# Fill pieces of a token mixer, traced at a lower scheduling priority than the delta rule they are mixed with

## The chip, the cores and the metric

The kernel runs on one core of a Trainium2 chip. It computes two transformer blocks, one behind the other, for one sequence of 256 tokens and a model width of 1024, all in float32. The metric is device time in microseconds; the kernel before takes 939.88 us (median of 3 runs, 939.13 to 941.12).

## The reference, cut to what matters

The change touches only the token mixer of the first block. The projection of the normed input is split into attention's q, k, v (8 heads of 64), the delta rule's q, k, v (`gdn_qkv`), a gate z and two scalars per head. Attention and the gated delta rule are independent of each other until `w_out` reads both.

```python
h = rms_norm(x, pre_mix_norm[l])
proj = jnp.einsum('bsd,dc->bsc', h, w_in[l])
att_q, att_k, att_v, gdn_qkv, gdn_z, gdn_a, gdn_b = jnp.split(proj, split_points, axis=-1)
o_att = moba_attention(...)          # one causal softmax block, relative bias
o_gdn = gated_deltanet(gdn_qkv, gdn_z, gdn_a, gdn_b, ...)
mix = jnp.einsum('bsc,cd->bsd', jnp.concatenate([o_att, o_gdn], axis=-1), w_out[l])
...
# gated_deltanet, chunks of 64 tokens (4 of them):
qkv = causal_depthwise_conv_silu(qkv, conv_w)
q = l2_normalize(q) * dh ** -0.5;  k = l2_normalize(k)
m = jnp.where(strict, jnp.einsum('bhnid,bhnjd->bhnij', k_beta, kc) * decay, 0.0)
uw = lax.linalg.triangular_solve(m + eye, rhs, lower=True, unit_diagonal=True)
attn_intra = jnp.einsum('bhnid,bhnjd->bhnij', qc, kc) * decay
def step(state, xs):                 # sequential over the 4 chunks
    v_new = u_c - w_c @ state
    o = q_c @ state + a_c @ v_new
    state = state * gl + k_c.T @ v_new
o = o * lax.rsqrt(jnp.mean(o * o) + EPS) * norm_w * silu(z)
```

The rest of the first block (an MLP of width 4096) and the whole second block follow and are as before.

## The kernel before, in words

**Weights.** Every large product is computed in three float32r passes: a weight tile arrives by DMA (`raw`, L214, 512 KB, issued by SyncE), ScalarE writes its rounded high part (`wh`), VectorE the rest (`wl`), and TensorE multiplies `wh` with the activations' high and low parts and `wl` with the high part. The buffers rotate: 3 of `raw`, 6 each of `wh` and `wl`. So a DMA for a weight tile can be issued when the tile three places earlier has been split, and a `wh` can be written when TensorE has used the one six places earlier.

**Two streams.** The mixer is written as two streams. The main stream is the delta rule, written out in `body` from the call `go(FILL[0])` on: gates, normed k and q, the product matrix, a triangular solve (blocks of 16 by GpSimd, `tb` and `ub`, through DRAM; then two levels, 16 and 32, by TensorE), `us` and `wt` from the solved matrix, and the scan over four chunks. The other stream is the generator `fill()`: the projections for conv q, k, v (`qkv(i)`), attention's q and k (`att_in`), z, v (`v_in`), attention's logits, softmax, transposed probabilities and output, and two steps of `w_out`. The main stream calls `go(amount)` between its own steps; `go` pulls pieces out of `fill()` until their planned microseconds (the yielded numbers) reach the amount, or until a named point ("k", "q", "v", "z") is passed. The table `FILL` holds the amounts.

**What sets the order.** The instructions are traced into a framework that schedules them: it gives each traced instruction a priority number that counts up (`tc.cur_priority`), simulates the engines with its own estimates, and writes a fixed list for each engine, at each step the instruction with the lowest number among those it takes for ready. On the chip each engine runs its list in that order. `issue_after` (the helper `after`, L171) pins a few instructions behind others.

**Names.** A tile's name ends in a trace counter. `mm_`, `sd_`, `at_` are PSUM banks: `mm` (3 banks) for projections, `sd` (3) for the delta rule, `at` (2) for attention. In the order: `raw_254`, `raw_257`, `raw_260`, `raw_267` and their `wh_`, `wl_` are z's four weight tiles (outputs `mm_252`, `mm_253`); `raw_281`, `raw_284` are those of attention's second k (`mm_280`); `raw_320` and so on v's (`mm_318`, `mm_319`). `aqk` are attention's q and k, `lg` its logits and probabilities, `pt` the transposed probabilities, `mixh`, `mixl` its output split for `w_out` (`mm_350` to `mm_352` and `at_353`, which keeps one of the two `at` banks from then on). `m` is the product matrix, `md` its copy in DRAM, `mb` its blocks on GpSimd, `td`, `ud` the solved blocks in DRAM, `T`, `U` what is read back, `Q` the middle products of a solve level, `st` the state, `ro` and `og` the output's norm and the output.

**The steps that the prediction speaks of.** GpSimd's block solve is L898 to L905; its result is written at L906 and L907 and read back at L954. The two levels are the loop at `for si, s in enumerate((16, 32))`, `us` and `wt` the loop behind it, and the scan the loop `for t in range(2)` behind `late = iter(())`; `gdn_out` normalises one half of the output. Attention's `logits`, `probs_T` and `att_out` are called only from `fill()`.

Of the kernel before, what the change touches and what calls it, by code (L numbers as in the profile page):

```python
# [31 lines left out]
TAIL_R = ((0, 3), (1, 3))  # L32
TAIL_O = ((0, 5), (1, 5))
YR_OFF = 1
WBUFS = 6
RBUFS = 3
GATE_H = ("sq", "xh", "xh")
# [62 lines left out]
def body(ctx: ExitStack, tc: tile.TileContext, I: dict, cst: bass.AP, out: bass.AP, dbg=None):  # L100
# [16 lines left out]
    def nm(s):  # L117
        uid[0] += 1
        return f"{s}_{uid[0]}"
# [51 lines left out]
    @contextmanager  # L171
    def after(what):

        if what in last:
            with tc.issue_after(last[what].ins):
                yield
        else:
            yield
# [33 lines left out]
    def load_w(w, k0, nk, c0, ncol):  # L212
        raw = wpool.tile([P, nk, ncol], F32, tag="raw", name=nm("raw"), bufs=RBUFS)
        last["ld"] = nc.sync.dma_start(raw, w[k0 * P:(k0 + nk) * P, c0:c0 + ncol].rearrange("(k p) n -> p k n", p=P))  # L214
        H = wpool.tile([P, nk, ncol], F32R, tag="wh", name=nm("wh"), bufs=WBUFS)
        L = wpool.tile([P, nk, ncol], F32R, tag="wl", name=nm("wl"), bufs=WBUFS)
        n = len(started)
# [50 lines left out]
    def put_off(f, n):  # L268

        later.append([n, f])  # L270
# [418 lines left out]
    def go(what):  # L689

        while what not in passed if isinstance(what, str) else what > 0:
            c = next(side, None)
            if c is None:
                return
            if isinstance(c, str):
                passed.add(c)
            elif not isinstance(what, str):
                what -= c
# [7 lines left out]


    go(FILL[0])
    load_consts(0, NMIX)
    pc = sdps()  # L710
# [5 lines left out]
    last["ld"] = nc.sync.dma_start(raw, w_in[:, 3584:3600].rearrange("(k p) n -> p k n", p=P))  # L716
    HL = wpool.tile([P, 8, 32], F32R, tag="wh", name=nm("wh"), bufs=WBUFS)
    with after("xh"):
# [34 lines left out]
    dump("beta", beta)  # L753

    go("k")
    last["yk"] = last["y"]

# [21 lines left out]
    mm(pg[:, 16:32], C("aft"), g)  # L779
    mm(pg[:, 32:64], ones, gm)  # L780
    go(FILL[1])

    def tok_major(i0, t):
# [404 lines left out]
    def yr_T(h):  # L1188
        yr.grow(4, "yr", "tg")
        for j in range(2):  # L1190
            ps = sdps()
            for i in range(2):
                f = 2 * j + i
                for t in range(2):
                    nc.tensor.transpose(ps[:, i * S + t * P:i * S + (t + 1) * P],  # L1195
                                        RN[t][h][:, f * P:(f + 1) * P], ident)
            for i in range(2):
                f = 4 * h + 2 * j + i
                v = ps[:, i * S:(i + 1) * S]
                hv, lv = yr.at(f)  # L1200
                act(hv, v, AF.Copy, scale=gret(f))
                stt(lv, v, gret(f), hv.bitcast(F32), MUL, SUB)

    for h in range(4):
# [22 lines left out]
        if h:  # L1227
            yr_T(h - 1)
    put_off(lambda: yr_T(3), YR_OFF)

# [155 lines left out]
```

## Time and profile before

| | |
|---|---|
| time, median of 3 runs | 939.88 us |
| profiled execution: time / span | 941.93 / 940.0 us |
| mean granted clock of TensorE | 0.993 |
| TensorE busy | 913.8 us (97%) |
| VectorE / ScalarE / GpSimd busy | 559.6 (60%) / 453.2 (48%) / 94.4 us (10%) |
| TensorE on the chain that ended last | 86% |

The mixer is the first fifth of the span: the first transposes of the normed input for the MLP come at 197.8 us. A time is read against the profiled execution's span and what lies around it (1.9 us). In a timeline, "idle before <-releaser" tells how long the engine had nothing to run and what ended that.

### The profile page before, as it was taken

What the parts mean: (1) busy time and instruction counts of PE and PEld (TensorE: products, weight loads), DVE (VectorE), ACT (ScalarE), POOL (GpSimd) and SP (SyncE); (2) the same over time, 40 slices, a digit from 0 to 9 for tenths busy, and PEclk for the clock granted to TensorE, in tenths of its full rate; (3) what the DMA queues carried; (4) which work ended last, traced back from release to release, by engine and by line L of the source; (5) the groups of instructions that cost most, each with busy time, mean ns of one, the idle gap of its engine ahead of it and who ended that gap; (6) DMA issues with size and microseconds to landing.
All of it is one profiled execution on the core that took longest, in us unless ns stands there. A gap on an engine that the chain in (4) does not pass through costs nothing.

```text
span 940.0 us, 15151 instructions
## 1 busy us (share of the span) xinstructions
PE 913.8 (97%) x6096; PEld 812.4 (86%) x6096; DVE 559.6 (60%) x770; ACT 453.2 (48%) x639; POOL 94.4 (10%) x127
## 2 busy tenths in 40 slices
PE   7797999999999999999999999999999999999997
PEld 7697887778999888799988899988888789999886
DVE  3776535486766544768666675645457656555443
ACT  4744464256655443654545554345344545444432
POOL 4187001130000000203200000000000000000000
PEclk9999899999999999999999999999999999999999
DMA  8685542156765666577645466566474567665551
GB/s 216 183 198 148 146 157 90 45 162 174 215 189 190 215 192 197 155 217 210 181 115 176 133 176 184 163 209 191 157 235 142 172 194 201 186 187 185 182 177 45
DMA packets 176870, 161.98 MB, mean 172 GB/s; under 512 B 18916, under 2 KB 144152, under 8 KB 176800
## 3 DMA queue, kind: packets, MB, share of 16 engines
q1 hardware_dynamic: 174912, 155.96, 56.6%
q0 software_dynamic: 1728, 4.78, 1.6%
q8 instruction: 48, 0.79, 0.4%
q10 hardware_dynamic: 160, 0.27, 0.1%
q14 instruction: 22, 0.18, 0.0%
HBM read 158.07 MB, written 2.92 MB: 171 GB/s over the span
## 4 chain that ended last, share of the span: by engine, by line
PE 86%; DMA 4%; DVE 4%; ACT 2%; issue 2%; POOL 1%; SPq 0%; POOLq 0%; ACTq 0%; DVEq 0%
PE mm L230 71%; PE at L230 8%; PE sd L230 7%; DMA raw<-in_w_in_dram 3%; DVE wl L149 1%; DVE acc L152 1%; ACT wh L146 1%; PE sd L802 1%; DMA hs<-in_dec_b_dram 1%; DMA raw<-in_w_up_dram 1%; ACT junk L405 0%; PE sd L1195 0%; POOL r L410 0%; POOL rnk L149 0%; POOL rnq L149 0%
## 5 line engine op out<-in xcount | busy, mean ns | idle before, releaser
L149 DVE TENSOR_TENSOR wl<-raw,wh 128x1024 fp32r<-128x1024 f32 x285 | 348.4, 1227 | 263.5 <-ACT wh L146 262.2
L146 ACT ACTIVATE wh<-raw 128x1024 fp32r<-128x1024 f32 x287 | 302.2, 1056 | 352.3 <-PE mm L230 125.6
L230 PE MATMUL mm<-xTh,wh 128*128 128x256 f32 x960 | 273.1, 286 | 0.2
L230 PE MATMUL mm<-xTl,wh 128*128 128x256 f32 x960 | 272.4, 285 | 0.3 <-DVE xTl L475 0.2
L230 PE MATMUL mm<-xTh,wl 128*128 128x256 f32 x960 | 268.8, 285 | 0.0
L230 PEld LDWEIGHTS mm<-xTl,wh 128*128 128x128 f32 x960 | 185.3, 193 | 1.6 <-DVE xTl L475 0.7
L230 PEld LDWEIGHTS mm<-xTh,wh 128*128 128x128 f32 x960 | 185.2, 193 | 0.8 <-ACT xTh L474 0.6
L230 PEld LDWEIGHTS mm<-xTh,wl 128*128 128x128 f32 x960 | 183.4, 193 | 0.7 <-issue 0.5
L230 PE MATMUL mm<-wh,xTh 128*128 128x512 f32 x264 | 104.0, 394 | 1.2 <-ACT xTh L394 1.2
L230 PE MATMUL mm<-wh,xTl 128*128 128x512 f32 x264 | 103.2, 391 | 1.5 <-DVE xTl L397 1.5
L230 PE MATMUL mm<-wl,xTh 128*128 128x512 f32 x264 | 103.3, 391 | 0.0
L230 PE MATMUL mm<-wh,hidh 128*128 128x512 f32 x162 | 63.3, 391 | 0.1
L230 PE MATMUL mm<-wl,hidh 128*128 128x512 f32 x162 | 63.3, 391 | 0.0
L230 PE MATMUL mm<-wh,hidl 128*128 128x512 f32 x162 | 63.0, 389 | 0.0
L230 PEld LDWEIGHTS mm<-wh,xTl 128*128 128x128 f32 x264 | 49.6, 188 | 12.9 <-DVE xTl L397 2.8
L230 PEld LDWEIGHTS mm<-wh,xTh 128*128 128x128 f32 x264 | 49.6, 188 | 12.3 <-ACT xTh L394 1.9
L230 PEld LDWEIGHTS mm<-wl,xTh 128*128 128x128 f32 x264 | 49.6, 188 | 10.4 <-DVE wl L149 0.5
L410 POOL TENSOR_TENSOR r<-ms,neghalf 128x1 f32<-128x1 f32 x13 | 9.8, 757 | 462.0 <-DVE ms L152 462.0
L230 PEld LDWEIGHTS mm<-wh,hidl 128*128 128x128 f32 x162 | 30.4, 188 | 6.4
L230 PEld LDWEIGHTS mm<-wh,hidh 128*128 128x128 f32 x162 | 30.5, 188 | 6.3 <-issue 0.5
L230 PEld LDWEIGHTS mm<-wl,hidh 128*128 128x128 f32 x162 | 30.5, 188 | 5.6
L405 ACT ACTIVATE junk<-x 128x512 f32<-128x512 f32 x18 | 11.3, 626 | 18.7 <-DVE x L149 12.9
(374 smaller groups left out, 1149.8 us busy)
## 6 DMA issues: line engine op xcount, KB each, us to landing
raw<-in_w_in_dram SPq DMA_DIRECT2D x116, 512.0 KB, 4.5
raw<-in_w_up_dram SPq DMA_DIRECT2D x32, 512.0 KB, 4.5
raw<-in_w_down_dram SPq DMA_DIRECT2D x32, 512.0 KB, 4.3
raw<-in_w_ff_gate_dram SPq DMA_DIRECT2D x22, 512.0 KB, 4.0
raw<-in_w_ff_up_dram SPq DMA_DIRECT2D x22, 512.0 KB, 4.5
raw<-in_w_ff_down_dram SPq DMA_DIRECT2D x22, 512.0 KB, 3.6
raw<-in_w_r_out_dram SPq DMA_DIRECT2D x16, 512.0 KB, 3.8
raw<-in_w_out_dram SPq DMA_DIRECT2D x8, 512.0 KB, 3.5
```

Source lines behind the costliest of these rows:

```text
L146: nc.scalar.activation(o, i, f, **kw)
L149: (eng or nc.vector).tensor_tensor(o, a, b, op=op)
L152: nc.vector.scalar_tensor_tensor(o, a, s, b, op0=op0, op1=op1)
L230: nc.tensor.matmul(o, a, b, start=start, stop=stop)
L405: last["sq"] = nc.scalar.activation(T2("junk", tag="j"), srcs[i], AF.Square, scale=1.0 / 32, accum_out=ss[:, i:i + 1])
L410: last["pow"] = nc.gpsimd.tensor_tensor(r, ms, neghalf[:, :1], op=ALU.pow)
L802: nc.tensor.transpose(ps[:, a * P:(a + 1) * P], src[:, a * P:(a + 1) * P], ident)
```

## The change

Each time `go` asks the fill generator for its next piece, it first raises the framework's priority counter by 4000 and lowers it again afterwards. Everything that the piece traces (loads, splits, matmuls, evictions, attention's vector work) so gets a number 4000 higher, behind every instruction of the delta rule; the counter at the end of the mixer is near 2100. What is computed, the pieces, their amounts and the buffers are as before.

```diff
 YR_OFF = 1
+LOW = 4000
 WBUFS = 6
...
         while what not in passed if isinstance(what, str) else what > 0:
+            tc.cur_priority += LOW
             c = next(side, None)
+            tc.cur_priority -= LOW
             if c is None:
```

The number of matmuls is the same; ScalarE gets two more table loads (ACT_TABLE_LOAD) in the mixer. Order differs on all engines from the start of the mixer to its end, and hardly behind it. Three places show how.

SyncE's list, where the solved blocks (`td`, `ud`) are written and read back (`U`, `T`), before:

```order
L906 DMA td_451<-tb_147_751 128x16x16
L907 DMA ud_452<-ub_148_752 128x16x16
L214 DMA raw_257_1400<-in_w_in_dram 128x2x512
L214 DMA raw_260_1418<-in_w_in_dram 128x2x512
L214 DMA raw_267_1474<-in_w_in_dram 128x2x512
L954 DMA U_213_1140<-ud_452 64x8x64 x2
L954 DMA T_212_1139<-td_451 64x8x64 x2
```

and now:

```order
L909 DMA td_451<-tb_147_751 128x16x16
L910 DMA ud_452<-ub_148_752 128x16x16
L215 DMA raw_260_1418<-in_w_in_dram 128x2x512
L215 DMA raw_267_1474<-in_w_in_dram 128x2x512
L215 DMA raw_281_1547<-in_w_in_dram 128x8x128
L215 DMA raw_284_1577<-in_w_in_dram 128x8x128
L957 DMA U_213_1140<-ud_452 64x8x64 x2
L957 DMA T_212_1139<-td_451 64x8x64 x2
```

One weight load (`raw_257`) has moved ahead of the write, and two (`raw_281`, `raw_284`) have moved from behind the reads to ahead of them.

TensorE's list, from the second level of the solve (`sd_263`), before (36 matmuls of z come ahead of it, 12 stand between `sd_265` and `sd_272`, of which three are shown):

```order
L230 MATMUL sd_263_1436<-U_241_1333,b_152_792 64x64 x16
L230 MATMUL sd_265_1455<-U_243_1352,b_154_796 64x64 x16
L230 MATMUL mm_252_1380<-wh_268_1476,xTh_25_165 128x512
L230 MATMUL mm_252_1380<-wl_269_1477,xTh_25_165 128x512
L230 MATMUL mm_252_1380<-wh_268_1476,xTl_29_169 128x512
```

and now:

```order
L231 MATMUL sd_263_1436<-U_241_1333,b_152_792 64x64 x16
L231 MATMUL sd_265_1455<-U_243_1352,b_154_796 64x64 x16
L231 MATMUL sd_272_1496<-Q_264_1453,T_237_1295 64x64 x16
L231 MATMUL sd_274_1515<-Q_266_1472,T_239_1314 64x64 x16
L231 MATMUL sd_300_1647<-vb_200_1062,U_273_1513 64x64 x16
L231 MATMUL sd_303_1667<-U_273_1513,kbe_124_645 64x64 x8
L231 MATMUL sd_304_1677<-U_273_1513,kbe_124_645 64x64 x8
L231 MATMUL sd_305_1687<-vb_202_1069,U_275_1532 64x64 x16
L231 MATMUL sd_308_1707<-U_275_1532,kbe_126_649 64x64 x8
L231 MATMUL sd_309_1717<-U_275_1532,kbe_126_649 64x64 x8
L231 MATMUL sd_317_1736<-us_301_1664,kd_125_646 128x128 x4
L231 MATMUL sd_316_1735<-us_301_1664,at_180_914 64x64 x8
```

The level, `us`, `wt` and the scan's first chunk stand in one piece; before, fill matmuls stood between most of them.

TensorE's list at attention's last head pair (1, 1), from the second transposes of its probabilities (`at_365`) to its output (`at_368`), before:

```order
L632 MATMUL at_365_1955<-ident_80,lg1_339_1863 128x128 x2
L230 MATMUL sd_360_1945<-st_315_1732,qdt_174_876 64x128
L230 MATMUL sd_360_1945<-us_306_1704,at_183_935 64x64 x2
L802 MATMUL sd_375_2009<-ident_80,og_373_1985 128x128
L230 MATMUL at_368_1966<-pt0_346_1893,av_333_1831 64x256
```

and now:

```order
L633 MATMUL at_365_1955<-ident_80,lg1_339_1863 128x128 x2
L231 MATMUL at_368_1966<-pt0_346_1893,av_333_1831 64x256
L231 MATMUL at_368_1966<-pt1_347_1894,av_334_1833 64x128
L231 MATMUL at_368_1966<-pt0_362_1952,av_333_1831 64x256
L231 MATMUL at_368_1966<-pt1_363_1953,av_334_1833 64x128
```

The scan's matmuls (`sd_360`, `sd_375`) that stood between attention's steps, and five more in front of `at_365`, are gone from there; they stand some 200 rows earlier. Ahead of the rows shown stand the transposes `at_364`, behind them the other four matmuls of `at_368` and then `mm_350`, which reads `mixh_366`.

## Rows read from the trace of the kernel before

**Rows 1.** busy time by engine of two stretches (us from the span's start): engine busy (x instructions), then PEclk

```profile
84.00:99.50 15.50, 12.85 (x83) 11.61 (x80) 6.83 (x9) 6.30 (x11) 5.01 (x4) 0.83 1.03 235
99.50:190.50 91.00, 90.90 (x905) 74.81 (x905) 43.79 (x76) 39.59 (x79) 6.78 (x8) 0.99 0.32 100
```

**Rows 2.** the same view, of the two stretches of the front with the lowest clock

```profile
46.00:50.10 4.10, 4.10 (x21) 3.44 (x20) 4.10 (x9) 3.59 (x5) 2.61 (x3) 0.58 0.47 128
...
94.00:101.40 7.40, 7.22 (x52) 6.09 (x52) 4.13 (x10) 3.38 (x10) 0.00 (x0) 0.54 1.08 248
```

**Rows 3.** GpSimd's instructions in order of time: start, us, engine, line, operation, idle time before

```profile
68.03 0.23 POOL L149 TENSOR_TENSOR tmpb<-mb,tb 128x15 f32<-128x15 f32 x1 [1.65 <-DMA mb<-md]
...
83.38 0.62 POOL L905 COPY ub<-tb 128x256 f32<-128x256 f32 x1
```

**Rows 4.** SyncE's DMA issues in order of time (SPq: the queue)

```profile
84.03 0.90 SPq L907 DMA_DIRECT2D ud<-ub  x1
85.02 2.01 SPq L214 DMA_DIRECT2D raw<-in_w_in_dram  x3
88.30 1.29 SPq L954 DMA_DIRECT2D U<-ud  x2
```

**Rows 5.** ScalarE in order of time, 89 to 94 us

```profile
89.51 1.06 ACT L146 ACTIVATE wh<-raw 128x1024 fp32r<-128x1024 f32 x1 [6.57 <-DMA raw<-in_w_in_dram]
...
93.55 0.58 ACT L146 ACTIVATE aqk<-mm 128x512 f32<-128x512 f32 x1
```

**Rows 6.** TensorE in order of time, 92 to 128 us

```profile
94.18 2.77 PE L230 MATMUL at<-aqk,aqk 64*128 64x128 f32 x8 [2.65 <-ACT aqk L146]
...
99.53 1.89 PE L230 MATMUL sd<-U,b 64*64 64x64 f32 x32
```

**Rows 7.** ScalarE in order of time, around 50 us

```profile
49.10 1.28 ACT L548 ACT_TABLE_LOAD   x1 [0.22 <-DVE acc L152]
50.39 0.63 ACT L548 ACTIVATE y<-acc 128x512 f32<-128x512 f32 x1
```

**Rows 8.** all engines in order of time, 159 to 166.5 us

```profile
159.45 0.60 ACT L146 ACTIVATE sq<-sd 128x512 f32<-128x512 f32 x1 [2.48 <-PE sd L230]
...
163.07 0.67 DVE L1016 TENSOR_REDUCE oss<-sq 128x8 f32<-128x512 f32 x1
...
164.09 1.65 POOL L149 TENSOR_TENSOR ro<-ms,neghalf 128x8 f32<-128x8 f32 x1 [3.68 <-DVE rse L618]
...
165.78 0.69 DVE L149 TENSOR_TENSOR og<-sd,ro 128x512 f32<-128x512 f32 x1
```

**Rows 9.** all engines in order of time, 171 to 177 us

```profile
171.46 0.27 PE L631 MATMUL at<-ident,lg 128*128 128x128 f32 x1
...
172.34 0.58 ACT L146 ACTIVATE pt<-at 128x512 f32<-128x512 f32 x1
...
173.50 0.44 PE L632 MATMUL at<-ident,lg 128*128 128x128 f32 x2
...
173.98 0.38 ACT L146 ACTIVATE pt<-at 128x256 f32<-128x256 f32 x1 [1.05 <-PE at L632]
...
174.86 1.57 PE L230 MATMUL at<-pt,av 128*64 128x256 f32 x16
...
176.47 0.60 ACT L146 ACTIVATE mixh<-at 128x512 fp32r<-128x512 f32 x1 [2.11 <-PE at L230]
```

**Rows 10.** TensorE in order of time, 119.4 to 122.4 us

```profile
119.41 0.39 PE L230 MATMUL mm<-wl,xTh 128*128 128x512 f32 x1
119.64 0.39 PE L230 MATMUL mm<-wh,xTl 128*128 128x512 f32 x1
119.95 2.08 PE L230 MATMUL sd<-U,b 64*64 64x64 f32 x64
121.97 0.50 PE L230 MATMUL mm<-wh,xTh 128*128 128x512 f32 x1
122.30 0.39 PE L230 MATMUL mm<-wl,xTh 128*128 128x512 f32 x1
```

## The prediction

> **What bounds the kernel now.** I read the page first: TensorE is busy for 97% of the span and makes up 86% of the chain that ended last, so only what TensorE loses can change the time. The windows by stage come next. In the mixer's second half it has nothing to lose: 90.90 of 91.0 us are busy at a granted clock of 0.99 [rows 1]. The loss lies in front of that, between 84.0 and 99.5, with 12.85 of 15.5 us busy at a clock of 0.83 [rows 1]. The timeline of TensorE names it: it waits 2.65 us for `aqk`, attention's first q and k as ScalarE evicts them [rows 6], and after the wait the clock is 0.54, near the lower of its two levels (1.2 of 2.4 GHz), for 7.4 us [rows 2]. Work done there at 0.54 would take 4.0 us at the full clock, so 3.4 us go to the clock: 6.05 us with the wait. That is all a better order could win in the mixer.
>
> What the front itself waits for is a chain through other engines: GpSimd gets the product matrix's blocks at 68.03 and solves until 84.0 [rows 3], SyncE writes the result at 84.03, issues three weight loads, and reads `U` at 88.30 [rows 4]; TensorE starts the first level at 99.53 [rows 6]. The order decides what stands beside this chain and what behind it.
>
> **The change, term by term**, against the profiled execution, whose 941.93 us are 2.05 above the median of the runs.
>
> *The front.* Two things move against each other. On ScalarE `aqk` now stands behind two of the weight splits after the solve, not three: with a split at 1.06 us and a few tenths between two [rows 5], the wait of 2.65 shrinks by about 1.5, and attention's first logits go from 94.18 to 92.7. On SyncE the read of `U` is now queued behind two more weight loads. The second of these (`raw_284`) needs the buffer of `raw_260`, a load issued at 85.0 that lands some 4.5 us later (issue at 85.02 [rows 4], its first reader at 89.51 [rows 5]); the split takes ScalarE 1.06 and VectorE somewhat more, an estimate of 1.3. So that load goes out at about 92, the reads of `U` at 92.7 to 94.0 (1.29 for two, [rows 4]) instead of 88.30, and with the same 4.5 us they land at 97.2 to 98.5. TensorE, which comes 1.5 us earlier and has 5.35 us of work from 94.18 to 99.53 [rows 6], arrives at about 98.0: what attention gains, the read of `U` eats, and the start is at 98.5.
>
> To this comes what happens to the chain's beginning. The number of a fill piece is now behind every instruction of the delta rule, so ScalarE's list has a conv's `y` between the delta rule's two `ee`, with a table load on either side; the split of gates and k preparation loses the place it had. One table load takes 1.28 us, and `y` 0.63 [rows 7]: two loads and a `y`, 3.2 us, stand in a queue that `kt` and `ee` pass, mostly beside other work. GpSimd had waited 1.65 us for its blocks [rows 3], so the chain has no slack there; what arrives late at 68.03 ends late at 84. I take 1.2 of the 3.2 us for the delay, and keep as ends 0 (the delta rule's own steps, now first, make up for it) and 4 (3.2 and a handover each way). The first level so starts at 99.7 instead of 99.53: +0.2, with ends of −1.5 (`U` is there in time and the 1.5 us stay won) and +4.
>
> The Trainium skill (ScalarE: Activation LUTs, "What ACT_TABLE_LOAD costs") gives a switch 2.66 us: 1283 ns for the load and about 1380 ns of drain. The row agrees with the load, and shows no drain behind it: `y` starts 0.01 us after the load's end [rows 7], and before it ScalarE was idle 0.22 us. With the drain the two extra loads would be an estimated 5.3 us and not 2.6, the delay 3.9 and not 1.2, and the sum 2.7 higher.
>
> *Solve and scan in one piece.* Before, fill matmuls stood between most of the steps of the second level, `us` and `wt`, and the scan; now they follow each other, and a step's eviction can be hidden only by the other half's step. A level's 16 small matmuls of one half take about 1.0 us (32 took 1.89, [rows 6]), an eviction 0.6 (as `sq`, [rows 8]): two halves that alternate just about cover each other. I take 0.3 (half an eviction) for one that stands behind attention's exponentials on ScalarE. The scan has a longer gap: VectorE's list now has `us` of the second half behind `og` of the first, and `og` needs `sq` (0.60), `oss` (0.67), `ro` on GpSimd (1.65) and itself (0.69) [rows 8]; `us` is an instruction like `og`, and an estimate of 0.6 goes to handovers and small steps: 4.9 us. TensorE has for that 10 fill matmuls at 0.23 [rows 10], one `sd` run of about 1.0 and the turns between, together 3.6. So 1.3 us of waiting, and with the 0.3 it is +1.6; ends 0 (all covered) and 3.6 (one more wait of 2, as long as the eviction and its queue).
>
> *Attention's tail.* This I trust most. Before, eight groups of the scan's matmuls stood from `at_364` to `at_368` of the last head pair; now none does. The second transposes must wait until `pt0` is out of its bank, for `at_353` holds the other one: from the transposes' end at 171.73 to `pt0`'s at 172.92, 1.2 us. Then the output waits for `pt1`: from 173.94 to 174.36, 0.4. Then `mm_350` waits for `mixh`: from 176.43 to 177.07, 0.6 [rows 9]. With 0.05 for each handover it is 2.4 from end to end; but a matmul's row runs on for 0.16 us beside the next one's start (119.41 and 0.39, next at 119.64, [rows 10]), an overlap that each of the three waits loses, so 2.8. Earlier in that tail three banks change hands between logits, output and probabilities in the same way: 0.8, an estimate of two waits like `pt1`'s, with ends 0 and 1.5. Sum +3.6, ends 2.4 and 4.3. The cover itself is not lost work: it runs earlier, in place of fill matmuls that now stand last.
>
> *Turns between the two kinds of work.* From the scan on TensorE's list has 20 runs of delta-rule work where it had 14. Each costs about 0.18 us: the run of 64 starts 0.31 after its predecessor instead of 0.23, and the fill matmul behind it is followed after 0.33 instead of 0.23 [rows 10]. Six of them are 1.1; some fall into waits already counted, so +0.6, ends 0 and 1.1.
>
> *The clock.* I leave the low stretch after the front as it is: TensorE still waits there, for `U` if not for `aqk`. That the waits in the scan or in the tail bring the clock down once more is not in the sum; it is a rival.
>
> *The sum:* 0.2 + 1.6 + 3.6 + 0.6 = 6.0. The execution would take 947.9, and a median 2.05 less: 945.9 us. The ends: −1.5 + 0 + 2.4 + 0 = 0.9 gives 940.8, and 4 + 3.6 + 4.3 + 1.1 = 13 gives 952.9; all at one end is unlikely, so the forecast's own range is 943 to 950.
>
> **The rivals.**
>
> *The clock falls once more* (0.17). The waits of the tail lie within 6 us of each other, and those of the scan come between short matmuls. For it: one wait of 2.65 us was enough for 7.4 us at 0.54 [rows 2, 6], and around 46 us the clock is 0.58 although TensorE is busy for all of 4.10 us [rows 2]. Against it: the single waits are 0.5 to 1.3 us. It costs 3.4 more: 949.3, and twice that if in both places, 952.7. The Trainium skill (TensorE: Matmul & The Clock Gate, "HAM oscillation — how this bites in real kernels") tells of the same thing, a loop whose waits for data bring the clock down again and again; the trace agrees in kind, with the 0.54 behind the one wait.
>
> *Nothing to measure* (0.13). The order differs in many places, but TensorE's amount of work does not, and the next weight tiles, loaded early now, may fill the waits of scan and tail; then the front's +0.2 and the turns' 0.6 remain: 940.7. Against it: a list is fixed, and behind `at_365` stands nothing that could go ahead.
>
> *Faster* (0.10). The loss that the front has, 6.05 us, goes altogether: with the delta rule's instructions first, `U` arrives before attention's logits are through, `aqk` comes in time, and the clock stays up; of the costs only the three waits of the tail, 2.8, remain: 939.88 − 6.05 + 2.8 = 936.6. It decides where the later waits stay below 6.05. For it: the whole wait hangs on three splits that ScalarE makes in a row [rows 5]. Against it: SyncE's list puts the reads of `U` behind more loads, not fewer.
>
> **How the numbers follow.** The forecast has 0.60. A measurement of this kernel can tell 0.2%, 1.9 us, so "same" is 938.0 to 941.8. Slower is the forecast and the clock's fall: 0.77; same the second rival with 0.13; faster 0.10. For 8 in 10 the range goes from 939.5, which leaves out the third rival and a part of the second, to 952.
>
> **What would show it.** In the profile after: the first `U` issued at 92 or later, with its first reader at 99 to 100; VectorE's `us` of the second half behind `og`, TensorE waiting for it about 1 us; the transposes at `at_365`, `at_368` and `mm_350` each waiting for ScalarE, 2.4 to 2.8 in all; TensorE's busy share in the 91 us behind the first level falling from 99.9% to about 94 to 96%. The forecast is wrong if `U` is issued before 90, if the mixer's end for TensorE is not later than now, or if a second low stretch of the clock shows behind the scan.

## The result, and the profile after

The changed kernel takes 951.11 us (median of 4 runs, 948.77 to 956.84), the kernel before 940.07 beside it: 1.0124 times as long, with an interval of 1.0096 to 1.0151, so 9 to 14 us slower. The side was forecast and the time lies in the range (939.5 to 952), but 5.2 us above the forecast of 945.9 and outside the forecast's own range of 943 to 950. The profiled execution took 950.85 us, its span is 948.9 at a mean granted clock of 0.986; before it was 940.0 at 0.993. The span is 8.9 us longer.

The windows by stage say where. The columns are those of [rows 1]; the two stretches are the front, up to about the middle of the first level, and the rest of the mixer. First the kernel before, then the changed one:

```profile
0.00:110.00 110.00, 94.46 (x894) 86.09 (x894) 65.23 (x131) 59.52 (x101) 50.50 (x74) 0.95 0.70 180
110.00:200.00 90.00, 89.48 (x733) 72.03 (x730) 49.21 (x83) 42.47 (x85) 8.86 (x11) 1.00 0.32 99
```

```profile
0.00:110.00 110.00, 96.63 (x782) 87.26 (x784) 65.44 (x130) 61.53 (x101) 51.35 (x74) 0.92 0.71 187
110.00:200.00 90.00, 84.81 (x808) 68.10 (x804) 40.00 (x71) 36.10 (x73) 6.73 (x8) 0.96 0.26 81
```

What TensorE lost in a stretch is its idle time (length less busy time) and what the clock took (busy time times one less the clock). Before: 15.5 idle and 4.7 for the clock in the front, 0.5 and 0 behind it. After: 13.4 and 7.7, then 5.2 and 3.4. So the front lost 2.2 us less by waiting and 3.0 more by the clock; solve, scan and tail lost 4.7 more by waiting and 3.4 more by the clock. That is 8.9 in all, the whole difference of the spans. (The clock has two decimals here, so each of its terms is good to half a microsecond.)

**The front.** GpSimd's solve, which started at 68.03 with its blocks [rows 3], starts 2.4 us later, and the write of `ud` comes 1.6 later than the 84.03 of [rows 4]:

```profile
70.39 0.65 POOL L150 TENSOR_TENSOR tmpb<-mb,tb 128x15 f32<-128x15 f32 x1 [1.62 <-DMA mb<-md]
```

The table loads that the order showed stand between the two `ee` on ScalarE. None is followed by a pause, and the second `ee` starts 3.4 us behind the end of the first. Before, it started at 48.26, so it comes 4.2 us later now; the solve comes 2.4 later. The first line is of the kernel before, the others of the changed one:

```profile
48.26 0.62 ACT L146 ACTIVATE ee<-ea 128x512 f32<-128x512 f32 x1
...
48.45 0.62 ACT L147 ACTIVATE ee<-ea 128x512 f32<-128x512 f32 x1
49.23 1.28 ACT L549 ACT_TABLE_LOAD   x1 [0.16 <-DVE acc L153]
50.53 0.63 ACT L549 ACTIVATE y<-acc 128x512 f32<-128x512 f32 x1
51.17 1.28 ACT L147 ACT_TABLE_LOAD   x1
52.47 0.63 ACT L147 ACTIVATE ee<-ea 128x512 f32<-128x512 f32 x1
```

On SyncE the four loads behind the write of `ud` (one line, 7.62 us, most of it waiting for a buffer) hold the read of `U` until 94.14; before it went out at 88.30 [rows 4], and the forecast had 92.7 and 1.2 of delay, 93.9:

```profile
85.64 0.69 SPq L910 DMA_DIRECT2D ud<-ub  x1
86.43 7.62 SPq L215 DMA_DIRECT2D raw<-in_w_in_dram  x4
94.14 1.29 SPq L957 DMA_DIRECT2D U<-ud  x2
```

ScalarE waits for the first of these loads until 91.34, then needs two splits, not three, and has `aqk` at 93.74, 0.2 later than before [rows 5]; TensorE, which reached that point 2.2 us earlier, waits 5.00 us instead of 2.65 [rows 6]. The first two instructions of the first level start at 99.66 (99.53 before), but the other thirty of the first half follow only from 102.65 on, behind fill matmuls at the low clock:

```profile
91.34 1.06 ACT L147 ACTIVATE wh<-raw 128x1024 fp32r<-128x1024 f32 x1 [8.04 <-DMA raw<-in_w_in_dram]
...
93.74 0.58 ACT L147 ACTIVATE aqk<-mm 128x512 f32<-128x512 f32 x1
```

```profile
94.37 2.93 PE L231 MATMUL at<-aqk,aqk 64*128 64x128 f32 x8 [5.00 <-ACT aqk L147]
...
99.66 0.47 PE L231 MATMUL sd<-U,b 64*64 64x64 f32 x2
...
102.65 1.14 PE L231 MATMUL sd<-U,b 64*64 64x64 f32 x30
```

**The scan.** On VectorE `us` of the second half runs behind `og`, as the order said; the norm's steps take the durations of [rows 8] to within 0.02 us:

```profile
135.73 0.69 DVE L150 TENSOR_TENSOR og<-sd,ro 128x512 f32<-128x512 f32 x1 [1.83 <-POOL ro L150]
136.33 0.67 DVE L150 TENSOR_TENSOR us<-us,sd 64x512 f32<-64x512 f32 x1
```

**TensorE's waits** in scan and tail, each with its releaser: 0.98 for `us`, 1.45 for the last `og`, and for the tail's two `pt` and `mixh` 1.25, 0.47 and 0.69, against 1.2, 0.4 and 0.6 read out of [rows 9]:

```profile
137.06 1.16 PE L231 MATMUL sd<-us,kd 64*128 64x128 f32 x8 [0.98 <-DVE us L150]
...
163.78 0.63 PE L805 MATMUL sd<-ident,og 128*128 128x128 f32 x4 [1.45 <-DVE og L150]
...
187.51 0.44 PE L633 MATMUL at<-ident,lg 128*128 128x128 f32 x2 [1.25 <-ACT pt L147]
188.42 1.57 PE L231 MATMUL at<-pt,av 128*64 128x256 f32 x16 [0.47 <-ACT pt L147]
190.68 0.50 PE L231 MATMUL mm<-wh,mixh 128*128 128x512 f32 x1 [0.69 <-ACT mixh L147]
```

**The clock.** Four stretches at or near the lower level, three in the front and one in the scan; before there were those of [rows 2]. The one in the scan is the first behind the front. The clock falls there at about 139.6, 2.5 us after the end of the wait for `us`, in a run of small matmuls without a gap, and rises at 146.6 in fill matmuls that are busy all the time. The two earliest stretches lie behind waits too (1.80 us until 19.47, 1.98 until 78.12), but behind the wait of 1.45 for `og` and the tail's three the clock stays up:

```profile
20.00:25.00 5.00, 5.00 (x31) 5.00 (x31) 2.36 (x10) 2.98 (x6) 0.00 (x0) 0.66 1.14 324
78.40:81.60 3.20, 3.20 (x18) 3.20 (x16) 2.60 (x4) 2.05 (x3) 2.75 (x6) 0.50 0.00 0
94.40:102.20 7.80, 7.80 (x30) 6.62 (x31) 5.62 (x13) 4.14 (x10) 0.00 (x0) 0.50 1.16 217
138.80:146.70 7.90, 7.90 (x33) 5.56 (x32) 0.30 (x1) 0.00 (x0) 0.00 (x0) 0.57 0.21 66
```

**Other executions.** Each execution's span and mean granted clock are known, though only one is profiled. What the clock took is at most span times (1 − clock), which counts a low clock in idle time too (for the changed kernel 950.0 × 0.0122 = 11.6); the rest is work and waits. Times are medians, the other columns means over the executions:

| kernel (executions) | time | clock | clock's part | rest |
|---|---|---|---|---|
| before (53) | 939.66 to 940.66 | 0.9932 | 6.4 | 931.4 |
| changed (4) | 951.11 | 0.9878 | 11.6 | 938.4 |
| front as changed, rest as before (9) | 942.55 | 0.9906 | 8.9 | 932.3 |
| changed behind z only (4) | 950.07 | 0.9868 | 12.6 | 935.3 |
| scan's waits taken away (4) | 949.61 | 0.9875 | 11.9 | 935.7 |
| tail's order changed, second try (4) | 950.24 | 0.9892 | 10.2 | 938.2 |
| all repairs, second try (8) | 943.66 | 0.9937 | 5.9 | 935.6 |
| before, writes by GpSimd (10) | 935.96 | 0.9949 | 4.8 | 929.8 |

By this count the change costs 7.0 us of waits and work and 5.2 of clock. The profiled pair above has 2.5 and 6.4: the profiled execution of the changed kernel has the smallest rest of its four (935.6, the others 938.3 to 940.5), and that of the kernel before a larger one (933.4) than any of the 53 (929.0 to 933.3).

### The profile page after: what moved, and what is told of

It reads as the page before. It is cut to its first block, busy times and chain, and to the rows that moved or that the text cites. A ratio compares the mean times of both kernels' runs of the same rounds, so it can differ in the third digit from the quotient of the medians.

```text
span 948.9 us, 15158 instructions
## 1 busy us (share of the span) xinstructions
PE 919.8 (97%) x6096; PEld 816.8 (86%) x6096; DVE 559.4 (59%) x770; ACT 455.6 (48%) x641; POOL 95.5 (10%) x127
## 4 chain that ended last, share of the span: by engine, by line
PE 80%; DVE 2%; issue 1%; ACT 1%; DMA 1%; POOL 1%; POOLq 0%; ACTq 0%; DVEq 0%
PE mm L231 67%; PE at L231 7%; PE sd L231 5%; DVE wl L150 1%; DMA raw<-in_w_up_dram 1%; POOL r L411 1%; ACT wh L147 0%; ACT junk L406 0%; DMA raw<-in_w_in_dram 0%; PE sd L805 0%; PE sd L1198 0%; POOL ro L150 0%; PE sd L1285 0%; PE sd L434 0%; DVE xs L422 0%
## 5 line engine op out<-in xcount | busy, mean ns | idle before, releaser
L231 PEld LDWEIGHTS mm<-wh,xTh 128*128 128x128 f32 x264 | 50.1, 190 | 12.6 <-ACT xTh L395 1.9
L150 POOL TENSOR_TENSOR rotl<-rot,roth 128x512 fp32r<-128x512 f32 x8 | 14.5, 1810 | 53.3 <-ACT roth L147 53.3
```

The source lines that it names most:

```text
L150: (eng or nc.vector).tensor_tensor(o, a, b, op=op)
L231: nc.tensor.matmul(o, a, b, start=start, stop=stop)
```

## The experiments

**Which part costs: front, back, or both.** Three kernels change the condition under which a piece gets the lower priority.

e1, lower only in front of z:

```diff
-            tc.cur_priority += LOW
+            low = LOW if "z" not in passed else 0
+            tc.cur_priority += low
```

> The fill pieces have the lower priority only up to the point z (conv, attention's first q and k, first logits, z); behind it they are numbered as before. Theory A (the loss lies behind z: waits in scan and tail and one more fall of the clock): the front's part alone costs 0 to 3 us, so 940 to 943, with TensorE's wait for aqk still near 5 us. Theory B (the loss lies in front, where the wait for aqk went from 2.7 to 5.0 us and the clock is low after it): 945 to 950.

Measured: 949.01 (944.04 to 957.44), ratio 1.0138 (1.0066 to 1.0211). By the words of the expectation this speaks for theory B, but the edit doesn't separate the parts. The pieces behind z, numbered as before, now stand ahead of the lowered pieces of z, so the order behind z is neither that of before nor that of the change: TensorE waits there for `mixl` (1.0 and 0.6 us), which neither of them shows. The third kernel below keeps the order behind z.

e2, lower only behind z (`low = LOW if "z" in passed else 0`):

> The lower priority only behind the point z (v, attention's probabilities and outputs, w_out, the later logits). Theory A: nearly all of the change's cost, 945 to 950, with the waits for us, og, pt and mixh of the profile after and a second low stretch of the clock. Theory B: 940 to 943. If the second low stretch is not there and the waits are, 944 to 946.

Measured: 950.07 (943.96 to 955.21), ratio 1.0117 (1.0051 to 1.0183). The waits are those of the profile after (1.1 for `us`, 1.4 for `og`, 1.2, 0.5 and 0.7 in the tail), and there are two low stretches behind the first level, one between 145 and 155 and one from about 165:

```profile
46.00:51.00 5.00, 5.00 (x21) 4.13 (x19) 4.45 (x9) 4.41 (x7) 3.92 (x3) 0.50 0.40 108
...
97.00:102.00 5.00, 5.00 (x42) 4.12 (x42) 2.91 (x9) 1.98 (x9) 0.00 (x0) 0.50 1.13 271
145.00:155.00 10.00, 9.21 (x49) 6.91 (x50) 4.17 (x8) 1.60 (x3) 0.00 (x0) 0.66 0.17 54
165.00:170.00 5.00, 5.00 (x19) 3.52 (x18) 2.49 (x6) 1.25 (x2) 0.00 (x0) 0.67 0.48 157
```

Three low stretches in the front belong to an order that is nearly that of before, so the front's clock can differ by as much as the change does to it where the order hardly differs.

e10, lower up to z, and behind z the same number added to both streams, so that they mix as before:

```diff
+            low = LOW if "z" not in passed else 0
+            tc.cur_priority += low
...
     go("z")
+    tc.cur_priority += LOW
```

> The front of the changed kernel and the rest of the kernel before: up to the point z the fill pieces are traced at the lower priority, and behind z both streams have the same added number, so that they mix as before. Theory A (the front gains 2 us of waits and gives them back in the clock; scan and tail carry the cost): 939 to 943, without waits for us, og, pt and mixh. Rival (the front part alone costs most, as the run with normal numbers behind z said): 946 to 950.

Measured: 942.55 (941.02 to 947.44, 9 runs), ratio 1.0033 (1.0016 to 1.0049), so 1.5 to 4.6 us. Behind the front TensorE is busy for 89.92 of 90 us at full clock; in the front it lost as long by waiting as before (15.5) and 7.6 to the clock, 2.9 more:

```profile
0.00:110.00 110.00, 94.46 (x746) 84.85 (x746) 65.51 (x130) 61.24 (x101) 51.89 (x74) 0.92 0.71 185
110.00:200.00 90.00, 89.92 (x870) 73.42 (x869) 46.80 (x80) 40.95 (x81) 8.75 (x10) 1.00 0.29 86
97.00:102.50 5.50, 5.50 (x21) 4.32 (x20) 3.18 (x6) 1.80 (x4) 0.00 (x0) 0.50 1.25 239
```

Theory A holds: about a quarter of the cost is the front's (0.33 of 1.24%), and in this profile that is clock; the rest needs the new order behind z, which with e2 costs nearly the whole by itself (0.5 to 1.8%).

**The scan's waits.** e5 puts `og` behind `us`, and the last output's norm and transposes at the lower priority:

```diff
+        with after("us2"):
             tt(h8(og), h8(po), hb(ro), MUL)
...
+    tc.cur_priority += LOW
     next(late)
+    tc.cur_priority -= LOW
```

> The changed kernel, with two waits of the scan taken away by order alone: VectorE's og of the first half stands behind us of the second half, and the last output's norm and transposes get the lower number too. The waits of TensorE for us (0.98) and for og (1.45) should be gone. Theory A (these waits also bring the clock down behind them): 943 to 947, with no low stretch between 130 and 170 us, and a higher mean clock. Rival (the low stretch is due to the many small matmuls of solve and scan, not to the waits): only the 2.4 us of waits go, 948 to 949, the low stretch stays.

Measured: 949.61 (946.89 to 952.06), ratio 1.0104 (1.0077 to 1.0131), which can't be told from the change's own 1.0124 (1.0096 to 1.0151). The two waits are gone, one of 1.07 for attention's logits is new, and the profile has no low stretch in the scan (clock 1.00 from 130 to 150); but another one stands at the tail's waits, where the profile of the change had none:

```profile
163.41 0.33 PE L631 MATMUL at<-ident,lg 128*128 128x128 f32 x1 [1.07 <-DVE lg L153]
```

```profile
130.00:150.00 20.00, 20.00 (x128) 15.01 (x127) 7.58 (x12) 6.56 (x9) 2.87 (x3) 1.00 0.16 48
186.00:192.00 6.00, 5.31 (x24) 3.94 (x23) 0.69 (x1) 0.60 (x1) 0.00 (x0) 0.55 0.36 105
```

In the table the rest falls by 2.7 (938.4 to 935.7) and the clock's part does not (11.6 and 11.9), each from four executions whose rests lie 4 to 5 us apart. So this run decides between neither theory: the time is near the rival's, the scan's clock is theory A's. Nor does it show that the waits brought the scan's low stretch: e9 below keeps both of them, and the clock stays at 1.00 there.

**The tail's waits.** e6 moves attention's last logits and probabilities next to v's matmuls:

```diff
         yield from probs_T(0, 1)
-        yield from v_in()
         yield from logits(1, 1)
-        yield from att_out(0)
         yield from probs_T(1, 0)
-        yield from w_out_steps(2)
+        yield from v_in()
         yield from probs_T(1, 1)
+        yield from att_out(0)
         yield from att_out(1)
+        yield from w_out_steps(2)
```

> The changed kernel, with the last pieces of the fill in another order: attention's logits and probabilities of the last head pair before and behind v's matmuls, both outputs next to each other, w_out's two steps last. Theory A: the three waits of the tail (1.25 for pt, 0.47 for pt, 0.69 for mixh, 2.4 in all) fall to under 1, 947 to 949. If the tail's waits also bring falls of the clock in some executions: 944 to 947. Rival (TensorE waits there for something else, v or the weights): 950 to 952.

Measured: 953.45 (951.11 to 954.07), ratio 1.0143 (1.0127 to 1.016). A new wait at the mixer's end cost more than the tail's: the steps of `w_out` have the lower priority, the rest of `w_out` has not, so the second step came last and nothing covered the first token half's norm:

```profile
210.77 1.11 PE L434 MATMUL sd<-ident,xs 128*128 128x128 f32 x4 [5.60 <-DVE xs L424]
```

e9 leaves the two steps of `w_out` between the two attention outputs (the edit is shown against e6):

```diff
         yield from att_out(0)
+        yield from w_out_steps(2)
         yield from att_out(1)
-        yield from w_out_steps(2)
```

> The changed kernel, with attention's last probabilities moved next to v's matmuls as in the earlier order of the fill, but w_out's two steps left between the two attention outputs, so that they do not fall behind the rest of w_out. Theory A: of the tail's 2.4 us of waits the two for pt (1.7) go, no new wait of 5 us at the mixer's end; 948 to 950. Rival (they come back elsewhere, or the clock falls as often): 950 to 952.

Measured: 950.24 (948.73 to 951.83), ratio 1.0115 (1.009 to 1.0141). The rival's case: the waits changed their names and not their sum, 3.1 us here against 2.4:

```profile
178.26 0.30 PE L631 MATMUL at<-ident,lg 128*128 128x128 f32 x1 [0.74 <-DVE lg L621]
...
180.29 1.57 PE L231 MATMUL at<-pt,av 128*64 128x256 f32 x16 [0.96 <-ACT pt L147]
182.55 0.50 PE L231 MATMUL mm<-wh,mixh 128*128 128x512 f32 x1 [0.69 <-ACT mixh L147]
...
190.47 0.50 PE L231 MATMUL mm<-wh,mixh 128*128 128x512 f32 x1 [0.69 <-ACT mixh L147]
```

With nothing but attention left at the end, another order among its steps moves the wait from one eviction to another. What covered them before was the scan.

The same profile bears on the clock. The scan's order is that of the change, with its waits of 0.98 for `us` and 1.44 for `og`, and still there is no low stretch behind the front:

```profile
110.00:200.00 90.00, 84.42 (x838) 67.58 (x839) 39.87 (x71) 35.85 (x73) 6.72 (x8) 1.00 0.28 83
```

So a fall of the clock behind these waits is a matter of the execution, and its absence in one profile is no proof that an edit removed it.

**The front's wait.** In the kernel before, and in the changed one, the weight loads that `aqk` needs stand on SyncE behind the write of the solved blocks. Four kernels let GpSimd issue that write:

```diff
-    nc.sync.dma_start(in_blocks(td), tb)
-    nc.sync.dma_start(in_blocks(ud), ub)
+    nc.gpsimd.dma_start(in_blocks(td), tb)
+    nc.gpsimd.dma_start(in_blocks(ud), ub)
```

e3 does it to the kernel before:

> The kernel before with one thing moved: the two writes of the solved blocks to DRAM are issued by GpSimd, which makes them, and not by SyncE, so that no weight load is queued behind a write that waits for the solve. Theory A (the front's wait for aqk comes from weight loads that SyncE holds back behind the write): the wait of 2.65 us goes and with it the slow clock after it, 3.4 us: 934 to 937. Rival (the loads are bound by their buffers or by DMA, or U takes over as the bound): 939 to 942.

Measured: 935.96 (935.14 to 939.51, 10 runs), ratio 0.997 (0.9948 to 0.9991). None of the loads stands behind the write any more; TensorE does not wait for `aqk`, and the clock stays at 1.00 where it was 0.54 [rows 2]. The new bound is the read of `U`, 2.3 us later than before, with 0.69 of waiting:

```profile
70.08 15.44 SPq L214 DMA_DIRECT2D raw<-in_w_in_dram  x6
90.61 1.29 SPq L954 DMA_DIRECT2D U<-ud  x2
```

```profile
90.74 1.57 PE L230 MATMUL at<-aqk,aqk 64*128 64x128 f32 x8
...
93.75 0.33 PE L230 MATMUL sd<-U,b 64*64 64x64 f32 x2
94.77 1.14 PE L230 MATMUL sd<-U,b 64*64 64x64 f32 x30 [0.69 <-DMA U<-ud]
```

```profile
84.00:94.00 10.00, 10.00 (x79) 9.26 (x76) 8.97 (x8) 3.88 (x4) 6.80 (x6) 1.00 0.50 119
94.00:101.40 7.40, 6.71 (x121) 6.16 (x119) 3.31 (x8) 3.79 (x11) 0.00 (x0) 1.00 0.90 206
```

e4 does it to the changed kernel:

> The changed kernel with the same edit: GpSimd issues the writes of the solved blocks. SyncE's list has three weight loads that wait for buffers ahead of the reads of U. Theory A: the wait of 5.0 us for aqk goes, and the reads of U are the bound of the first level; 943 to 948. Rival (the reads of U are held back even more by the third load): 950 to 953.

Measured: 948.63 (944.82 to 951.11, 9 runs), ratio 1.0089 (1.0063 to 1.0116), just above theory A's range. The wait for `aqk` is gone, one of 3.43 for `U` stands in its place:

```profile
98.04 0.44 PE L231 MATMUL sd<-U,b 64*64 64x64 f32 x2 [3.43 <-DMA U<-ud]
```

e8 is e3 with two weight loads put behind the reads of `U` (`with after("U")` around the issue of `raw_281` and `raw_284`):

> The kernel before with the writes issued by GpSimd, and in addition two weight loads behind the reads of U. TensorE still waited 0.7 us for U with the writes moved alone. Theory A: that wait goes, 934.5 to 935.5. Rival: attention's second k, whose weights these loads are, comes later and is waited for: 937 to 940.

Measured: 937.04 (934.33 to 940.67, 10 runs), ratio 0.9972 (0.9954 to 0.9991). The wait for `U` did not go (2.0 us in its profile): the reads are held back by the write's landing (issued at 86.40, landed 4.2 us later, first read at 90.69) and not by the loads. Against e3 nothing can be told.

e13 is the front of e10 with both edits of e8:

> The front of the changed kernel, the rest as before, and the writes of the solved blocks issued by GpSimd with two weight loads behind the reads of U. Theory A (the long wait for aqk is the front's only cost): 933 to 937, as the kernel before with the writes moved, or 1 us below it. Rival (the clock falls in the front all the same, behind the wait for the transposed q, as it did in the run with all repairs): 937 to 941.

Measured: 938.51 (935.76 to 941.6, 10 runs), ratio 0.9994 (0.9981 to 1.0008): no change from before, and no better than e3. The time is in the rival's range, but not for the rival's reason: no low stretch follows the wait for the transposed q in its profile, and the mean clock of the ten is that of before (0.993). The longest wait of its profile is the one for `U`:

```profile
95.94 0.30 PE L232 MATMUL sd<-U,b 64*64 64x64 f32 x2 [3.55 <-DMA U<-ud]
```

**All repairs together.** e7 is the changed kernel with the edits of e5, e6 and e8:

> The changed kernel with all repairs: GpSimd issues the writes of the solved blocks, two weight loads stand behind the reads of U, the scan's two waits and the tail's three are taken away by order. Theory A (the change's cost is these waits and the clock that they bring down): 934 to 939, at or below the kernel before with the writes moved (935.96). Rival (a further cost hangs on solve and scan in one piece, such as the turns between the two kinds of matmul): 940 to 945.

Measured: 947.3 (946.46 to 948.82), ratio 1.0084 (1.0069 to 1.0099), with the wait at the mixer's end (5.19) that e6 had made. e12 has e9's order instead of e6's:

> The changed kernel with all repairs, with w_out's two steps left between the attention outputs: the wait of 5.2 us at the mixer's end, which the earlier version of this had, should be gone. Theory A: 939 to 943, with a sum of waits below that of the kernel before and a clock that stays lower (0.988 to 0.991). Rival (the loss is of another kind than waits and clock): 945 to 948.

Measured: 943.66 (941.12 to 945.51, 8 runs), ratio 1.0043 (1.0028 to 1.0059). That lies between the two ranges: of the change's 1.24% two thirds are repaired. Its profile shows a wait of 1.91 for the transposed q, and from there 14 us at 0.54 in which TensorE is never idle:

```profile
82.53 0.66 PE L806 MATMUL sd<-ident,qd 128*128 128x128 f32 x4 [1.91 <-ACT qt L147]
```

```profile
84.00:98.00 14.00, 14.00 (x101) 12.37 (x98) 7.43 (x16) 4.74 (x11) 9.16 (x13) 0.54 0.40 75
0.00:110.00 110.00, 98.66 (x844) 88.63 (x846) 64.95 (x131) 60.98 (x102) 55.87 (x76) 0.94 0.68 183
110.00:200.00 90.00, 86.39 (x772) 69.22 (x767) 46.25 (x77) 39.85 (x80) 9.07 (x10) 0.98 0.28 86
```

But that stretch is not what is left of the cost. In the front as a whole this execution loses less than the kernel before: 11.3 idle and 5.9 for the clock, against 15.5 and 4.7. Behind it the loss is 3.6 idle and 1.7 for the clock, against 0.5 and 0. The idle time there is attention's, which the repairs left or moved (1.07 and 0.98 us, and twice 0.69). Over the eight executions the clock is not lower than before either (0.9937 and 0.9932).

## Why the prediction was right in side and too low

- **The front** (+0.2 forecast). The read of `U` (93.9 forecast, 94.14) and the first level's start (99.7, 99.66, though only for two of its matmuls) came as worked out. One step of it failed: the wait for `aqk` did not shrink by 1.5 but grew to 5.00. The split less that was counted is there, but the loads stand behind a write that comes 1.6 later, and TensorE, which had waited 4.5 us less up to that point, ran out of fill earlier. By the profiled pair it is 0.8 (−2.2 of waits, +3.0 of clock), by e10 1.5 to 4.6. That 0.8 is near the forecast's 0.2 is luck: two changes that were not foreseen nearly cancel.
- **The delay of the solve** (1.2, ends 0 and 4) was 2.4 at its start and 1.6 at its end. The Trainium skill's drain behind a table load (ScalarE: Activation LUTs, "What ACT_TABLE_LOAD costs") would have made it 3.9; in the profile after `y` and `ee` start 0.02 us behind their loads.
- **Solve and scan, tail, turns** (+1.6, +3.6, +0.6: 5.8). Measured 4.7 of idle time behind the front, where TensorE's busy share is 94.2% from 110 to 200 (94 to 96 forecast). The wait for `us` (1.3 forecast, 0.98) and the tail's three (2.4 from end to end, 2.41) were right one by one. Not foreseen was the wait of 1.45 for the last `og`, whose transposes also moved ahead; the 0.8 in the earlier tail and the 0.3 of an eviction behind exponentials hardly show. The turns' 0.6 were not measured by themselves; the profiled pair leaves nothing for them. The 1.0 us for a level's 16 matmuls was read from a run at the lower clock: the 1.89 of [rows 6] lie in the stretch at 0.54 of [rows 2], and 64 such matmuls took 2.08 at the full clock [rows 10], so 16 take about 0.5. It did no harm, since the profile after has no wait in the levels.
- **The clock** is the step that failed: "I leave the low stretch after the front as it is", and a further fall "is not in the sum; it is a rival". The rival's price of 3.4 is what the scan's low stretch took (7.9 us at 0.57), and its 949.3 is nearer to the measured 951.11 than the forecast is. It should have been the likelier of the two: a change that adds five waits to a program whose clock falls behind some of its waits can be expected to add clock losses too. The front's clock (+3.0) was in no case at all. The signs that the prediction named for itself came, and the mixer's end is later (the transposes behind it start at 207.16, before at 197.81). Of the signs against it one nearly came: the further low stretch, in the scan and not behind it.
- **The sum.** In the profiled pair the waits, forecast at 6.0 with the turns, came to 2.5, and the clock, forecast at nothing, to 6.4. Over all executions it is 7.0 and 5.2. By either count the clock is the missing term. By the profiled pair the waits were sized too large as well, and the two faults offset each other, so it is in part luck that the forecast comes within 5.2 us.
- **Nothing to measure** and **faster** fell: the front's 6.05 us are to be had in part (e3 gains 0.9 to 4.9 by its ratio), but through the write's queue; the change itself made that wait longer.

What stays open: the rest in the table, span less clock, differs by up to 5 us between executions of the changed kernel (935.6 in the profiled one, 940.5 in the longest), and in e12 it is 4.2 above the kernel before although in its profiled execution it is no larger than in that of the kernel before (932.8 against 933.4). Which wait grows in the executions that were not profiled is not known. Of the table's 7.0 us of waits and work the profiled pair shows 2.5; where the rest lies is open. Nor is it shown what decides at which of the waits the clock falls in a given execution.

## What to carry to other kernels

A lower priority for filler takes it away from the place where it was cover: what the scheduler runs first finishes early, and the last part of the program is then only filler with its own latencies. Before such a change, list what each stream's last steps would wait for once they are alone, and count for each new wait a possible fall of the clock. A queue that issues both loads and a write that waits for a long computation deserves a look by itself: moving the write to another queue brought 0.3% (0.1 to 0.5%), when the whole reordering brought a loss.

## What the runs showed of the hardware that was not expected

One and the same program differs from execution to execution by the clock: 53 executions of the kernel before have mean granted clocks of 0.989 to 0.999 and spans of 932.3 to 940.6 us, and the two shortest have the two highest clocks. The clock is not all of it, since span less the clock's part still goes from 929.0 to 933.3. A write of 128 KB to DRAM that SyncE issued landed 3.1 to 4.2 us later (before and after); issued by GpSimd it took 4.2 to 6.2 (4.2 and 6.0 in e3, 6.2 and 6.0 in e4, 4.2 in e8, 4.3 in e13), and each of the two issues kept GpSimd itself for 1.2 us. A wait can be followed by a fall of the clock in one kernel's profile and not in another's: behind the wait of 0.98 for `us` the clock fell in the profile after and stayed up in e9's. And TensorE at the lower clock can be busy without a gap: in e12 for 14 us on end.
